# Output projection's second pass: reading S3's result ahead of the weight differences and the second half of the row combinations one product later; gate's S2 blocks split one step later

## The chip, the cores and the metric

The kernel runs on one core of one Trainium2 chip. The metric is the device time of one execution in microseconds (us), as the median of several runs of the same program; less is better. A separate execution was recorded by the hardware profiler; every row of a profile below comes from it. Engines are named as in the profile: PE is TensorE's matmul, PEld its weight load, DVE is VectorE, ACT is ScalarE, POOL is GpSimd, SP is SyncE, which here only issues transfers. A name with a q (SPq, ACTq) is the instruction queue of such an engine in a row about issues or waits.

## The reference

One decoder layer on 1024 tokens of 2048 features, all in float32. The part up to `mixed` is done before the place of the change; the change lies in the last lines but one.

```python
hn = rmsnorm(h, norm_mix_g[i])
proj = hn @ w_in[i]                       # q, k, v, gate columns of two head groups
...                                       # stick-breaking and differential attention
mixed = jnp.concatenate([sb_out * jax.nn.silu(sb_g), df_out * jax.nn.silu(df_g)], axis=-1)
h = h + mixed @ w_out[i]                  # 1024x2048 @ 2048x2048

gate = jax.nn.sigmoid(rmsnorm(h, norm_ple_g[i]) @ w_ple_gate[i])   # 2048x2048
h = h + gate * (p[i] @ w_ple_proj[i])     # 1024x256 @ 256x2048
...
return rmsnorm(h, norm_final_g)
```

## The kernel before

**Arithmetic.** All tiles hold features on the 128 partitions and 512 tokens (one half of the sequence) on the free axis. A float32 product is made of three matmuls of a shorter float format (fp32r): each operand is split into a high half, which ScalarE casts, and a low half, which VectorE gets by subtracting the high half from the original; TensorE then adds high by high, high by low and low by high into one accumulator.

**Seven products.** The projections and the gate go through a scheme of the Strassen kind (class `Seven`). The matrices are cut into two by two blocks, and instead of eight block products seven are made: A11 and A12, which take weight blocks as they are, S2, S1, S3 and S4, which take sums of operand rows (S1 to S4) and differences of weight blocks (T1 to T4) or a block itself, and A22, which takes T4. For the weights a block 12 is subtracted by a block 11 (T1), block 22 by T1 (T2), block 12 by 22 (T3), and block 21 by T2 (T4). Each product here is 12 matmuls of 128x512: four slices of the contraction, three matmuls each.

**The projection with w_out** runs in two passes over the contraction (`ph` 0 and 1) and in each over eight units (`u`), a unit being a group of 128 output features of each half. The second pass has seven products in a unit, in this order: A11, A22 of the unit before, S2, S4 of the unit before, A12, S1, S3. (Unit 7 has S3 ahead of S1.) Products of a unit are accumulated in few banks: S3 adds to the bank `b` in which S2 already lies, VectorE reads the two together as `u3 = b + s1` (L1912), and then A22 of the same unit accumulates into `b` again. The banks `b` and `c` bear the name `pbc`. The results, with what the first pass left (`hr`, read back from DRAM), are rows of the new h. `put` stores them to DRAM (`h_d`) from GpSimd and asks for their squares for the next RMSNorm: ScalarE squares (L1403), and for one half of the tokens GpSimd adds them up (`total`, L1404).

**The row combinations.** The gate needs sums of rows of h, S1 to S4, scaled with the norm's weights. The function `sums` makes them for one unit out of its four results and stores them to DRAM (`hcomb_d`). It has two halves: `one` (a ScalarE copy at L1791, VectorE's L1792 and L1794, two stores) and `two` (VectorE's L1798 and L1800, two stores). They are put into a list of deferred work, `soon`, with the number of the product after which they are to be issued: for units 0 to 5 at one and two products behind S4, for units 6 and 7 later.

**The step behind a product.** `prod` issues 12 matmuls and then calls `step`, which in this order: makes the high half of the next weights (`whigh`: for S2 and S3's places in the ring of weights it first subtracts T1 and T2, or T3, on VectorE at L764, and for A22 T4; then the cast on ScalarE at L799), calls `taken` (a function given by the caller, here the reading of S3's result), makes the low half (`wlow`, VectorE's L813), and runs the deferred work that is due. Weights are made one product ahead or more. A weight block's tile is loaded again from DRAM on SyncE's queue (`wload`, L1710 for the gate's, elsewhere for w_out's) as soon as its last reader has been issued; block 21 has one tile only, read by a cast and by T4.

**The gate** follows without a break. It takes its operands from `h_d` and `hcomb_d`: `gate_loads` issues the transfers at once and puts the splitting (cast at L684, low half later) into a queue `xq` with the earliest step. Its products are `gprod`: two steps of 12 matmuls each. Between them stands z, the embedding product of 12 matmuls with small weights `pwhl` (`ple`, L1859), whose cast at L1851 is issued by `plew` within `gate1`. `p1`, `p2` and `gate1` alternate: `p1(3)`, the loads of S2's first four blocks on ScalarE's queue, `p2(2)`, `gate1(0)`, `p1(4)`, `gate1(1)` and so on. ScalarE applies the sigmoid (L1990).

**The order of work.** On TensorE, VectorE and ScalarE the order is that in which the code issues the instructions in this stretch; each engine works its own list from top to bottom, and waits for other engines by semaphores. Transfers stand in the list of the engine that issues them. SyncE's and GpSimd's lists are set by a scheduler from the same program.

Of the kernel before, what the change touches and what calls it, by code (L numbers as in the profile page):

```python
# [70 lines left out]
def _body(ctx, nc, tc, ap):  # L71
# [551 lines left out]
    with tc.tile_pool(name="at", bufs=2) as at, ExitStack() as banks:  # L623
# [32 lines left out]
        class Seven:  # L656

            def __init__(self, w, n, flow):
                self.w, self.flow = w, flow
                self.units = [(ph, u) for ph in range(2) for u in range(n)]  # L660
                self.wq, self.XC, self.T = {}, {}, {}
                self.made, self.late, self.slot = [], 0, 0
                self.xq = deque()
                self.after = None
                self.soon, self.ended, self.calm, self.nlow = [], {}, False, 0
                self.extra, self.ticks = (), False
                self.ring, self.odd, self.opening = WRING, 1, list

            def places(self, place, nm):
# [163 lines left out]
            def step(self, taken=None):  # L833

                self.slot += 1
                self.whigh()
                if taken and not self.ticks:
                    taken()
                self.wlow()
                if self.slot in self.extra:  # L840
                    self.whigh()
                    self.wlow()
                self.due()
                if taken and self.ticks:
                    taken()
                for _ in range(3 if len(self.xq) > 8 and not self.calm else 2):
                    e = next((e for e in self.xq if e[0] <= self.slot), None)
                    if e:
                        self.xq.remove(e)
                        e[1]()  # L850

            def prod(self, u, ph, nm, o, start, taken=None):
                self.product(u, ph, nm, o, start, tick=self.ticks and bool(side.q))
                if u == 7 and self.ended:
                    for k in range(4):
                        del self.XC[nm, k]
                self.after(u, ph, nm)
                self.step(taken)
# [501 lines left out]
        def gate_operand(nm, i, eng):  # L1360

            hi, lo = op.places(GPLACE[nm][i], "g" + nm)
            src = {"A11": h_d[1, i], "A12": h_d[1, i + 8], "A22": h_d[0, i + 8]}.get(nm)
            if src is None:
                src = hcomb_d[SUMS.index(nm), i]
            gain = {"A11": i, "A12": i + 8, "A22": i + 8, "S3": i}.get(nm)
            if gain is not None:
                gain = gvec[:, 1, gain:gain + 1]
            if nm == "A12":
                with tc.issue_after(op.loaded.ins):  # L1370
                    eng.dma_start(lo.bitcast(F32), src)
            else:
                d = eng.dma_start(lo.bitcast(F32), src)
                if nm == "A11":
                    op.loaded = d
            return partial(op.split, "g" + nm, i, hi, lo, gain, apart=True)

        def gate_loads(nm, i0, n=4, eng=nc.sync):
            e = [(op.slot + (3 if nm in ("A11", "A12") else 2), gate_operand(nm, i0 + j, eng)) for j in range(n)]
            if nm == "A11" and i0 > 3:  # L1380
                xq.extendleft(reversed(e))
            else:
                xq.extend(e)
# [398 lines left out]
        def sums(u, hq, a2, b1):  # L1782

            a1, b2 = hq[:, 0, :], hq[:, 1, :]
            ga, ma, gb, mb = [g[:, k:k + 1] for k in (u, u + 8) for g in (gvec[:, 1, :], gneg)]

            def store(nm, v):
                nc.sync.dma_start(hcomb_d[SUMS.index(nm), u], v)

            def one():  # L1790
                A.activation(b2, b2, AF.Copy, scale=gb)  # L1791
                V.scalar_tensor_tensor(b2, a2, ga, b2, op0=ALU.mult, op1=ALU.add)  # L1792
                store("S1", b2)
                V.tensor_tensor(a2, a2, a1, op=ALU.subtract)  # L1794
                store("S3", a2)

            def two():
                V.scalar_tensor_tensor(a1, a1, ma, b2, op0=ALU.mult, op1=ALU.add)  # L1798
                store("S2", a1)
                V.scalar_tensor_tensor(b1, b1, mb, a1, op0=ALU.mult, op1=ALU.add)  # L1800
                store("S4", b1)

            return one, two
# [3 lines left out]
        def rest_of(st_, first):  # L1807

            u, ph, b, c, s1, u2, hq = st_
            nm, o_, t, hf, ch = ("A22", b, s1, 0, u) if first else ("S4", c, u2, 1, u + 8)  # L1810
            prod(u, ph, nm, o_, False)
            o = ftile()
            V.tensor_tensor(o, o_, t, op=ALU.add)
            put(o, ph, hf, ch)
            if ph == 1:
                hrows[u, hf] = o
                if not first:
                    lag = {6: 10, 7: 7}.get(u, 1)
                    op.soon.extend((op.slot + lag + i, fn) for i, fn in enumerate(sums(u, hq, hrows.pop((u, 0)), hrows.pop((u, 1)))))

        praws = []

# [38 lines left out]
                T.matmul(z, w[:, 1, k, :], ph[:, k, :], start=False, stop=k == 1)  # L1861

        for ph in range(2):
            op.ticks = not ph
            for u in range(8):
                r = {}
                for e in ((1, u + 8), (1, u), (0, u + 8), (0, u)) if ph else ():
                    r[e] = ev.tile([P, HALF], F32, name="hr", tag="xt", bufs=4)
                    nc.sync.dma_start(r[e], h_d[e])
                early = ph == 0 and u in s1s  # L1870
                s1 = s1s.pop(u) if early else ev.tile([P, HALF], F32, name="s1", tag="sq", bufs=2)
                if ph:
                    a = pp.tile([P, HALF], F32, name="pa", tag="acc", bufs=2)
                    prod(u, ph, "A11", a, True)
                    A.copy(s1, a)
                    if prev:
                        rest_of(prev, True)
                elif not early:
                    nc.sync.dma_start(s1, part_d[u])
                if ph == 0 and u % 3 == 0:  # L1880
                    b, c = [pp.tile([P, HALF], F32, name="pb", tag="acc", bufs=2) for _ in range(2)]
                elif ph == 1 and u == 7:
                    b = single("pbc")
                    c = None
                else:
                    b, c = single("pbc"), single("pbc")
                hq = at.tile([P, 2, HALF], F32, name="hq", tag="qz") if ph else None
                prod(u, ph, "S2", b, True)
                u2 = at.tile([P, HALF], F32, name="u2", tag="sg", bufs=3)
                V.tensor_tensor(u2, b, s1, op=ALU.add)  # L1890
                if ph:
                    V.tensor_tensor(u2, u2, r[1, u + 8], op=ALU.add)

                def p2():
                    prod(u, ph, "A12", a, False)
                    V.tensor_tensor(hq[:, 0, :], a, r[1, u], op=ALU.add)
                    put(hq[:, 0, :], ph, 1, u)

                if ph:
                    if prev:  # L1900
                        rest_of(prev, False)
                    p2()
                    if u < 7:
                        prod(u, ph, "S1", c, True)
                else:
                    if prev:
                        rest_of(prev, True)
                    prod(u, ph, "S1", c, True)
                    if prev:
                        rest_of(prev, False)  # L1910
                u3 = at.tile([P, HALF], F32, name="u3", tag="sg", bufs=3)
                prod(u, ph, "S3", b, False, lambda: V.tensor_tensor(u3, b, s1, op=ALU.add))  # L1912
                if ph:
                    V.tensor_tensor(u3, u3, r[0, u + 8], op=ALU.add)
                    if u == 7:
                        c = single("pbc")
                        prod(u, ph, "S1", c, True)
                o = hq[:, 1, :] if ph else ftile()
                V.tensor_tensor(o, c, u3, op=ALU.add)
                put(o, ph, 0, u + 8)  # L1920
                if ph:
                    V.tensor_tensor(s1, s1, r[0, u], op=ALU.add)
                prev = u, ph, b, c, s1, u2, hq
                if ph == 0 and 1 <= u < 5:
                    for nm, i in (("A11", u - 1), ("A12", u - 1)):
                        xq.append((op.slot + 3, load_operand(1, nm, i, A)))
# [495 lines left out]
```

## Time and profile before

| | |
|---|---|
| median of 3 runs | 2362.04 us (2360.44 to 2363.05) |
| profiled execution | 2361.19 us |
| its span, first to last instruction | 2359.4 us |
| mean granted TensorE clock | 0.997 |
| PE busy | 2317.2 us, 98% of the span, 11096 matmuls |
| PEld / DVE / ACT / POOL busy | 82% / 76% / 50% / 14% |
| chain of waits, by engine | PE 71%, DVE 12%, ACT 7%, DMA 6% |
| moved by DMA | 581.02 MB, mean 246 GB/s |

The span lies 1.8 us under the execution's own time: what stands around the first and the last instruction. In a row of a timeline the first number is the start in us from the start of the span, the second the duration in us, then engine, line, operation, output and inputs, and in brackets what the engine waited for ahead of it and how long. A row with x4 is four instructions of a kind in a row. In a row of the waits stand the microseconds in all, the number of waits and the longest. A row of windows has the stretch, its length, the busy times of PE, PEld, DVE, ACT and POOL with the number of instructions, the granted clock, the DMA engines' share of busy time, and GB/s. The second pass of the projection lies from about 1740 to 1985 us, unit by unit about 19 to 21 us apart; the gate follows.

### The profile page before, as it was taken

How to read it: one execution, taken by the hardware profiler on the slowest of the kernel's cores; microseconds unless marked ns; L12 is line 12 of the kernel's file. 1: busy time of each engine (PE TensorE's matmuls, PEld its weight loads, DVE VectorE, ACT ScalarE, POOL GpSimd, SP SyncE). 2: the span in 40 equal slices, each digit the busy share in tenths (PEclk: the TensorE clock that was granted, in tenths of full speed). 3: DMA queues.
4: the chain of work that ended last, by engine and by line, in shares of the span. 5: the costliest groups of instructions: out<-in, count | busy, mean ns of one | idle time of the engine just before them, and what ended most of it. 6: DMA issues, size and time to landing. Idle time of an engine off the chain costs nothing.

```text
span 2359.4 us, 32445 instructions
## 1 busy us (share of the span) xinstructions
PE 2317.2 (98%) x11096; PEld 1928.3 (82%) x11096; DVE 1789.8 (76%) x3123; ACT 1189.0 (50%) x2214; POOL 327.3 (14%) x480
## 2 busy tenths in 40 slices
PE   9999999999999999999999999999999999999997
PEld 7888888888888878887888888888878878788886
DVE  7489676666677787777888876767887877788778
ACT  6334243333367775445676764445633435533544
POOL 2211112332200000000001011011121232000000
PEclk9999999999999999999999999999999999999998
DMA  7699589999977788787656566677888778898666
GB/s 260 225 313 344 170 255 281 293 278 271 303 246 252 246 266 299 256 263 245 204 182 199 165 190 215 203 214 238 213 211 215 242 229 269 291 326 292 243 227 217
DMA packets 252725, 581.02 MB, mean 246 GB/s; under 512 B 28496, under 2 KB 41040, under 8 KB 252560
## 3 DMA queue, kind: packets, MB, share of 16 engines
q1 hardware_dynamic: 177952, 394.34, 49.7%
q0 software_dynamic: 55312, 149.71, 24.2%
q10 hardware_dynamic: 19296, 34.90, 4.3%
q8 instruction: 87, 1.43, 0.3%
q14 instruction: 78, 0.64, 0.1%
HBM read 373.32 MB, written 213.91 MB: 249 GB/s over the span
## 4 chain that ended last, share of the span: by engine, by line
PE 71%; DVE 12%; ACT 7%; DMA 6%; issue 3%; SPq 0%; ACTq 0%; DVEq 0%
PE acc L263 7%; PE acc L261 7%; PE acc L262 7%; PE pbc L708 6%; PE pbc L710 6%; PE pbc L709 6%; PE pa L708 2%; PE pa L710 2%; PE pa L709 2%; PE tp L480 2%; DMA wraw<-w_out 2%; PE pb L708 1%; PE pb L710 1%; PE pb L709 1%; PE pb L1941 1%
## 5 line engine op out<-in xcount | busy, mean ns | idle before, releaser
L799 ACT CAST wpr<-T 128x512 fp32r<-128x512 f32 x208 | 125.3, 621 | 440.3 <-DVE T L764 360.4
L261 PE MATMUL acc<-xh,whi 128*128 128x512 f32 x768 | 315.0, 410 | 0.0
L263 PE MATMUL acc<-xh,wlo 128*128 128x512 f32 x768 | 302.5, 394 | 1.5 <-DMA wlo<-wlo_d 1.4
L262 PE MATMUL acc<-xl,whi 128*128 128x512 f32 x768 | 301.0, 392 | 0.0
L263 PEld LDWEIGHTS acc<-xh,wlo 128*128 128x128 f32 x768 | 144.5, 188 | 36.2 <-DMA wlo<-wlo_d 3.6
L262 PEld LDWEIGHTS acc<-xl,whi 128*128 128x128 f32 x768 | 145.4, 189 | 24.0
L261 PEld LDWEIGHTS acc<-xh,whi 128*128 128x128 f32 x768 | 145.0, 189 | 23.4 <-DVE qk L1567 0.2
L799 ACT CAST wpr<-wraw 128x512 fp32r<-128x512 f32 x144 | 88.6, 618 | 146.9 <-DMA wraw<-w_vg 40.2
L813 DVE TENSOR_TENSOR wpr<-T,wpr 128x512 fp32r<-128x512 f32 x208 | 145.8, 701 | 9.2 <-ACT wpr L799 6.8
L936 POOL DMA_DIRECT2D vg_d<-hc x120 | 86.8, 724 | 328.4 <-DVE hc L1181 187.9
L503 DVE TENSOR_TENSOR awl<-tp,awh 128x256 fp32r<-128x256 f32 (+1 forms) x160 | 92.5, 578 | 42.8 <-ACT awh L498 42.2
L498 ACT CAST awh<-tp 128x256 fp32r<-128x256 f32 (+1 forms) x160 | 80.6, 504 | 82.6 <-PE tp L480 76.3
L813 DVE TENSOR_TENSOR wpr<-wraw,wpr 128x512 fp32r<-128x512 f32 x144 | 97.7, 686 | 23.5 <-ACT wpr L799 23.5
L321 DVE CUSTOM_DVE_ANT_0 z<-z,masks 128x512 f32<-128x512 f32 (+7 forms) x128 | 97.1, 769 | 23.0 <-PE z L341 14.0
L708 PE MATMUL pbc<-cS,wpr 128*128 128x512 f32 x288 | 112.0, 389 | 0.0
L709 PE MATMUL pbc<-cS,wpr 128*128 128x512 f32 x288 | 112.0, 389 | 0.0
L710 PE MATMUL pbc<-cS,wpr 128*128 128x512 f32 x288 | 112.0, 389 | 0.0
L373 DVE TENSOR_TENSOR_SCAN st<-pt 128x511 f32<-128x511 f32 (+3 forms) x64 | 86.7, 1354 | 27.2 <-ACT pt L366 26.8
L366 ACT ACTIVATE pt<-z 128x512 f32<-128x512 f32 (+3 forms) x64 | 41.8, 653 | 76.6 <-DVE z L349 74.6
L528 PE MATMUL av<-awl,v 128*128 128x256 f32 x256 | 73.4, 287 | 1.7 <-DVE awl L503 1.7
L526 PE MATMUL av<-awh,v 128*128 128x256 f32 x256 | 72.0, 281 | 0.7 <-ACT awh L498 0.7
L527 PE MATMUL av<-awh,v 128*128 128x256 f32 x256 | 72.2, 282 | 0.0
(589 smaller groups left out, 6816.5 us busy)
## 6 DMA issues: line engine op xcount, KB each, us to landing
wlo<-wlo_d SPq DMA_DIRECT2D x94, 512.0 KB, 5.2
whi<-whi_d SPq DMA_DIRECT2D x74, 512.0 KB, 4.1
wraw<-w_vg SPq DMA_DIRECT2D x129, 256.0 KB, 4.8
vg_d<-hc POOLq DMA_DIRECT2D x120, 256.0 KB, 5.7
wraw<-w_in SPq DMA_DIRECT2D x54, 512.0 KB, 5.3
wraw<-w_gate SPq DMA_DIRECT2D x92, 256.0 KB, 4.9
wraw<-w_out SPq DMA_DIRECT2D x72, 256.0 KB, 4.6
wlo_d<-wlo SPq DMA_DIRECT2D x34, 512.0 KB, 3.4
```

The source lines that it names most:

```text
L261: T.matmul(acc[c], hi[:, k2, kh, c, :], xh, start=first, stop=False)
L262: T.matmul(acc[c], hi[:, k2, kh, c, :], xl, start=False, stop=False)
L263: T.matmul(acc[c], lo[:, k2, kh, c, :], xh, start=False, stop=last)
L321: V.tensor_tensor_reduce(z, z, mwide[:, 0:n], -DF_SCALE, 3.0e38, ALU.add, ALU.min, mx)
L373: V.tensor_tensor_scan(st[:, off + 1:nkey], pt[:, off:nkey - 1], pt[:, off:nkey - 1], initial=1.0, op0=ALU.mult, op1=ALU.bypass)
L503: V.tensor_tensor(wl[:, o, :], tp[:, o, :], wh[:, o, :].bitcast(F32), op=ALU.subtract)
L708: T.matmul(o, wh[:, w], xh, start=start and k == 0, stop=False, skip_group_check=True)
L709: T.matmul(o, wh[:, w], xl, start=False, stop=False, skip_group_check=True)
L710: T.matmul(o, wl[:, w], xh, start=False, stop=k == 3, skip_group_check=True)
L799: A.copy(t[:, 0], src)
L813: V.tensor_tensor(t[:, 1], src, t[:, 0].bitcast(F32), op=ALU.subtract)
L936: G.dma_start(vg_d[hf, blk, u], o, **(dict(accum_op=ALU.add) if ph else {}))
```

## The change

Four edits, all in the order in which work is issued:

- In the projection's second pass (`op.first`), `step` calls `taken` ahead of `whigh`, not behind it: the reading of S3's result is issued before the next weights' differences.
- The second half of a unit's row combinations (`two`) is due two slots behind the first half instead of one, where the lag is 1 (the combinations of units 0 to 5, issued in units 1 to 6).
- In unit 7, where S1 follows S3, the reading of S1's result (now the function `second`) is given to `prod` as `taken`, instead of being issued after the whole step and after the sum with `r`.
- The gate's S2 blocks that ScalarE's queue loads first, `("S2", 0)`, may be split three steps after their issue, not two.

```diff
@@ -663,7 +663,7 @@
-                self.extra, self.ticks = (), False
+                self.extra, self.ticks, self.first = (), False, False
@@ -833,8 +833,10 @@
             def step(self, taken=None):
 
                 self.slot += 1
+                if taken and self.first:
+                    taken()
                 self.whigh()
-                if taken and not self.ticks:
+                if taken and not (self.ticks or self.first):
                     taken()
                 self.wlow()
                 if self.slot in self.extra:
@@ -1376,7 +1378,7 @@
         def gate_loads(nm, i0, n=4, eng=nc.sync):
-            e = [(op.slot + (3 if nm in ("A11", "A12") else 2), gate_operand(nm, i0 + j, eng)) for j in range(n)]
+            e = [(op.slot + (3 if nm in ("A11", "A12") or eng is A and (nm, i0) == ("S2", 0) else 2), gate_operand(nm, i0 + j, eng)) for j in range(n)]
@@ -1816,7 +1818,7 @@
                 if not first:
                     lag = {6: 10, 7: 7}.get(u, 1)
-                    op.soon.extend((op.slot + lag + i, fn) for i, fn in enumerate(sums(u, hq, hrows.pop((u, 0)), hrows.pop((u, 1)))))
+                    op.soon.extend((op.slot + lag + (1 + (lag == 1)) * i, fn) for i, fn in enumerate(sums(u, hq, hrows.pop((u, 0)), hrows.pop((u, 1)))))
@@ -1861,7 +1863,7 @@
         for ph in range(2):
-            op.ticks = not ph
+            op.ticks, op.first = not ph, ph
             for u in range(8):
@@ -1912,11 +1914,16 @@
                 prod(u, ph, "S3", b, False, lambda: V.tensor_tensor(u3, b, s1, op=ALU.add))
                 if ph:
                     V.tensor_tensor(u3, u3, r[0, u + 8], op=ALU.add)
-                    if u == 7:
-                        c = single("pbc")
-                        prod(u, ph, "S1", c, True)
                 o = hq[:, 1, :] if ph else ftile()
-                V.tensor_tensor(o, c, u3, op=ALU.add)
+
+                def second():
+                    V.tensor_tensor(o, c, u3, op=ALU.add)
+
+                if ph and u == 7:
+                    c = single("pbc")
+                    prod(u, ph, "S1", c, True, second)
+                else:
+                    second()
                 put(o, ph, 0, u + 8)
```

TensorE's and GpSimd's lists read the same before and after. Three places show what moves on the others. The line numbers of the changed kernel are two to seven higher there.

VectorE in a unit of the second pass, from the result of A12 to the result of S1. `hq` holds the unit's own results and, at L1798 (now L1800), those of the unit before; `u` is u3, `hc` a result of the unit before. Before:

```order
L1896 TENSOR_TENSOR hq<-pa,hr 128x512
L764 TENSOR_TENSOR T_18069<-wraw 128x512
L764 TENSOR_TENSOR T_18072<-wraw,T_18069 128x512
L813 TENSOR_TENSOR wpr<-wraw,wpr 128x512
L1798 SCALAR_TENSOR_TENSOR hq<-hq,gneg 128x512
L1800 SCALAR_TENSOR_TENSOR hc<-hc,gneg,hq 128x512
L1912 TENSOR_TENSOR u_18081<-pbc,s_17946 128x512
L813 TENSOR_TENSOR wpr<-T_18072,wpr 128x512
L1914 TENSOR_TENSOR u_18081<-u_18081,hr 128x512
L1919 TENSOR_TENSOR hq<-pbc,u_18081 128x512
```

After:

```order
L1898 TENSOR_TENSOR hq<-pa,hr 128x512
L764 TENSOR_TENSOR T_18069<-wraw 128x512
L764 TENSOR_TENSOR T_18072<-wraw,T_18069 128x512
L813 TENSOR_TENSOR wpr<-wraw,wpr 128x512
L1914 TENSOR_TENSOR u_18077<-pbc,s_17946 128x512
L813 TENSOR_TENSOR wpr<-T_18072,wpr 128x512
L1800 SCALAR_TENSOR_TENSOR hq<-hq,gneg 128x512
L1802 SCALAR_TENSOR_TENSOR hc<-hc,gneg,hq 128x512
L1916 TENSOR_TENSOR u_18077<-u_18077,hr 128x512
L1920 TENSOR_TENSOR hq<-pbc,u_18077 128x512
```

The two operations of `two` have gone behind the read of S3's result and one low half of weights. No difference of weights (L764) stands next to the read, before or after, so its place relative to those is unchanged in this unit; what has moved it is the edit of the slot.

ScalarE in the gate, around `gate1(0)`: the casts of weights (L799), of S2's operand blocks (L684, `cgS`), of the embedding's weights (`pwhl`), the sigmoid, and the copy behind `p1(4)`. Before:

```order
L799 CAST wpr<-wraw 128x512 x2
L684 CAST cgS_19147<-cgS_19147 128x512
L684 CAST cgS_19149<-cgS_19149 128x512
L1851 CAST pwhl<-pw 128x256
L799 CAST wpr<-wraw 128x512
L1990 ACT_TABLE_LOAD
L1990 ACTIVATE o<-o 128x512
L684 CAST cgS_19151<-cgS_19151 128x512
L684 CAST cgS_19153<-cgS_19153 128x512
L799 CAST wpr<-wraw 128x512
L2002 COPY s_19249<-paz 128x512
L2003 DMA part_d<-s_19249 128x512
```

After:

```order
L799 CAST wpr<-wraw 128x512 x2
L1853 CAST pwhl<-pw 128x256
L799 CAST wpr<-wraw 128x512
L1997 ACT_TABLE_LOAD
L1997 ACTIVATE o<-o 128x512
L684 CAST cgS_19147<-cgS_19147 128x512
L684 CAST cgS_19149<-cgS_19149 128x512
L799 CAST wpr<-wraw 128x512
L684 CAST cgS_19151<-cgS_19151 128x512
L684 CAST cgS_19153<-cgS_19153 128x512
L2009 COPY s_19247<-paz 128x512
L2010 DMA part_d<-s_19247 128x512
```

The first two S2 casts have gone behind the `pwhl` cast, the next weights' cast and the sigmoid; the third and fourth behind one more weight cast.

SyncE's list where the projection ends and the gate's loads begin. `cgA11l` are blocks of h for the gate's A11, `cgA12l` for A12, `wraw` the gate's weights. Before:

```order
L1710 DMA wraw<-w_gate 128x512
L1373 DMA cgA11l<-h_d 128x512
L1710 DMA wraw<-w_gate 128x512
L1710 DMA wraw_19487<-w_gate 128x512
L1710 DMA wraw<-w_gate 128x512
L1373 DMA cgA11l<-h_d 128x512
L1710 DMA wraw<-w_gate 128x512
L1371 DMA cgA12l<-h_d 128x512 x4
```

After:

```order
L1712 DMA wraw<-w_gate 128x512 x2
L1375 DMA cgA11l<-h_d 128x512 x3
L1712 DMA wraw<-w_gate 128x512 x2
L1712 DMA wraw_19487<-w_gate 128x512
L1712 DMA wraw<-w_gate 128x512 x2
L1375 DMA cgA11l<-h_d 128x512
L1373 DMA cgA12l<-h_d 128x512 x4
```

Ahead of the last `cgA11l` there now stand both weight loads that had one on each side of it, and three of the `cgA11l` are issued in a row.

## The prediction

> **What bounds the kernel now.** TensorE is busy nearly all the time, so I read first the list of waits on TensorE, to find the few that the change can reach.
>
> ```profile
> PE pbc L708 <- DVE u L1912: 3.5, 4, 1.5
> ```
>
> The columns are microseconds in all, times, and the longest. This is A22 of the projection's second pass: it accumulates into the bank that VectorE must first have read at L1912 (u3, the result of S3). Further down stands the small embedding product z in the gate, which waits for the cast of its weights:
>
> ```profile
> PE z L1859 <- ACT pwhl L1851: 1.5, 1, 1.5
> ```
>
> TensorE's timeline shows where the first wait falls (start, duration):
>
> ```profile
> 1861.02 0.39 PE L708 MATMUL pbc<-cA,wpr 128*128 128x512 f32 x1
> ...
> 1880.06 0.39 PE L708 MATMUL pbc<-cA,wpr 128*128 128x512 f32 x1
> ...
> 1920.34 0.50 PE L708 MATMUL pbc<-cA,wpr 128*128 128x512 f32 x1 [1.40 <-DVE u L1912]
> ...
> 1941.16 0.50 PE L708 MATMUL pbc<-cA,wpr 128*128 128x512 f32 x1 [1.46 <-DVE u L1912]
> ```
>
> A unit whose products are not held up takes 1880.06 - 1861.02 = 19.04 us. These are A22 after units 1, 2, 4 and 5. From 1880.06 to 1941.16 three units took 61.10 us, 3.98 more than 3 x 19.04. So the question is why VectorE falls behind by that much. Its own timeline, for unit 4 and the start of unit 5:
>
> ```profile
> 1913.70 1.28 DVE L1792 SCALAR_TENSOR_TENSOR hq<-hc,gvec,hq 128x512 f32<-128x512 f32 x1 [4.22 <-ACT hq L1791]
> ...
> 1918.15 0.74 DVE L1798 SCALAR_TENSOR_TENSOR hq<-hq,gneg 128x512 f32<-128x512 f32 x1
> 1918.93 0.75 DVE L1800 SCALAR_TENSOR_TENSOR hc<-hc,gneg,hq 128x512 f32<-128x512 f32 x1
> 1919.60 0.69 DVE L1912 TENSOR_TENSOR u<-pbc,s 128x512 f32<-128x512 f32 x1
> 1920.20 1.16 DVE L813 TENSOR_TENSOR wpr<-T,wpr 128x512 fp32r<-128x512 f32 x1
> 1921.29 0.68 DVE L1914 TENSOR_TENSOR u<-u,hr 128x512 f32<-128x512 f32 x1
> ...
> 1925.79 0.68 DVE L764 TENSOR_TENSOR T<-wraw,T 128x512 f32<-128x512 f32 x1
> ...
> 1934.52 1.28 DVE L1792 SCALAR_TENSOR_TENSOR hq<-hc,gvec,hq 128x512 f32<-128x512 f32 x1 [4.31 <-ACT hq L1791]
> ```
>
> TensorE resumed at 1920.34, 0.05 us after L1912 ended. From 1913.70 to 1925.79 VectorE stands still for nothing. The T at 1925.79 is T4; only when it has read block 21 may the next block 21 be loaded, and ScalarE's queue waits for that load:
>
> ```profile
> 1932.72 0.62 ACT L799 CAST wpr<-wraw 128x512 fp32r<-128x512 f32 x1 [4.55 <-DMA wraw<-w_out]
> ```
>
> Behind this cast, in ScalarE's order, stands L1791, and for that VectorE's next L1792 waits. This closes a loop: L1792, 12.09 us of VectorE work to T4, then 8.73 us of load and casts, L1792 again, 20.82 us in all. No step of it waits for TensorE. The loop, not the place of one read, is what is slower than 19.04 us.
>
> ```profile
> L1792 DVE SCALAR_TENSOR_TENSOR hq<-hc,gvec,hq x6: 1272/1276/1281, 1853.8 to 1954.1; 128x512 f32<-128x512 f32 x6
> ```
>
> The six L1792 of units 1 to 6 (durations in ns, first and last start): 100.3 us for five turns, 20.06 each.
>
> **The change part by part.** *u3 ahead of the row combinations (their second half one product later).* In units 1 to 6, L1798 and L1800 move behind L1912 and the following L813. L1912 can start where L1798 does, at 4.45 us after L1792 instead of 5.90: 1.45 us sooner. If the loop's turns keep their length, A22 after unit 6 is ready at 1954.11 + 4.45 + 0.69 + 0.05 = 1959.30. It now starts 0.05 us after L1912 as well, 1.45 us later. So the deadline is relieved once, by 1.45 us, and not in each unit: the waits do not go away, the loop runs late again. This is the upper end of that term if no turn becomes shorter.
>
> *What the move does to the turn.* GpSimd adds in the same place:
>
> ```profile
> 1919.49 1.33 POOL L1404 TENSOR_TENSOR total<-total,masks 128x512 f32<-128x512 f32 x1 [2.08 <-ACT masks L1403]
> ```
>
> L813 at 1920.20 overlaps this add and takes 1.16 us where the same subtraction's length elsewhere (L1914) is 0.68; it ends 0.54 us after the add. L1792 takes 1.28 against 0.74 of L1798. L1912, which reads the accumulator and one SBUF tile, lies wholly inside the add and keeps its 0.69. So the read of S3 covers about half of the add today. In the new order L1912 is at 4.45, L813 at 5.05, L1798 at 5.65 and L1800 at 6.4 after L1792, and the add is asked for at 5.79: it now meets only operations that it holds up. If L1798 has started, the add starts at its end near 6.3, lasts 1.3, and L1800 ends 0.54 us later, at 8.1; L1914 then starts at 8.05 instead of 7.59, 0.46 later in each turn. Bounds: 0.66 later (the add gets in ahead of L1798), 0.48 earlier (VectorE's back-to-back operations hold GpSimd off until L1914, so L813's present delay goes). I take 0.46, the case nearest to what the rows at L813 and L1792 show.
>
> [...]
>
> *The effect on the loop.* Five turns at +0.46 put L1792 of unit 6 at +2.3 us. A22 after unit 6 then starts at 1959.30 + 2.3 = 1961.6, 0.9 us later than now; in units 3 and 4 the 1.45 us still outweigh it.
>
> *Unit 7's S1 result read as soon as u3 is there.* On VectorE it passes one L813 and one L692. It removes at most about 0.3 us at S4 of unit 7, and this does not carry on (next part), so I cost it at nothing. "Read first" itself moves nothing in units 0 to 6: ahead of S3's step stands no weight difference on VectorE.
>
> *The loads at the seam.* SyncE's queue, before:
>
> ```profile
> 1980.11 0.33 SPq L1373 DMA_DIRECT2D cgA11l<-h_d  x1
> 1980.49 0.42 SPq L1710 DMA_DIRECT2D wraw<-w_gate  x1
> ```
>
> ```profile
> SPq L1373 <- DMA h_d<-hq: 3.7, 1, 3.7
> ```
>
> ```profile
> 1979.00:1981.00 2.00, 1.97 (x9) 1.33 (x8) 2.00 (x3) 1.29 (x3) 1.12 (x1) 1.00 0.08 30
> ```
>
> The last row's end is the DMA engines' busy share, 0.08, and GB/s: for two microseconds the engines are nearly empty, since the load at 1980.11 waits for a store of h to land. In the new order the weight load at 1980.49 stands ahead of it and fills the hole. That takes one 256 KB transfer out of the queue behind: at the page's mean rate 256 KB / 246 GB/s = 1.07 us, at a busier 300 or so 0.9; I take 0.9 sooner for the gate's loads.
>
> ```profile
> DMA packets 252725, 581.02 MB, mean 246 GB/s; under 512 B 28496, under 2 KB 41040, under 8 KB 252560
> ```
>
> *The gate's S2 blocks one step later.* ScalarE before:
>
> ```profile
> 2026.70 1.15 ACT L799 CAST wpr<-wraw 128x512 fp32r<-128x512 f32 x2 [2.73 <-DMA hc<-h_d]
> 2028.77 1.27 ACT L684 CAST cgS<-cgS 128x512 fp32r<-128x512 f32 x2 [0.93 <-DMA cgS<-hcomb_d]
> 2029.94 0.40 ACT L1851 CAST pwhl<-pw 128x256 fp32r<-128x256 f32 x1
> 2031.37 0.63 ACT L799 CAST wpr<-wraw 128x512 fp32r<-128x512 f32 x1 [1.03 <-DMA wraw<-w_gate]
> ...
> 2036.38 0.41 ACT L1851 CAST pwhl<-pw 128x256 fp32r<-128x256 f32 x1 [0.40 <-ACT s L2002]
> ```
>
> and TensorE, the held z, the product behind it, and the product behind the next z:
>
> ```profile
> 2030.40 0.50 PE L1859 MATMUL z<-ph,pwhl 128*128 128x512 f32 x1 [1.49 <-ACT pwhl L1851]
> ...
> 2031.90 0.40 PE L1939 MATMUL paz<-cgA12h,wpr 128*128 128x512 f32 x1
> ...
> 2039.13 0.39 PE L1939 MATMUL paz<-cgA11h,wpr 128*128 128x512 f32 x1
> ```
>
> The first pwhl is freed from the two S2 casts and can be done at 2028.2, so this wait goes. But the casts go from ScalarE's idle time to behind 2031.37, which waits for its own load; the next pwhl then ends 1.1 us later, at 2036.38 + 1.1 + 0.41 = 2037.9. With 0.05 for the release and 1.50 for a held z (2030.40 to 2031.90) the next product starts at 2039.45 instead of 2039.13. The wait moves to the next z, and what is left is 0.3 us of loss, whatever TensorE had gained before it, plus what the gate's loads have moved.
>
> *Sum.* At this z: loop +2.3 (the sixth turn's 0.46 falls into the two empty microseconds), weight load -0.9, second pwhl +0.3: +1.7 us. Behind it the DMA engines are full (row below; share 1.00 over 50 us), so what comes later passes on this shift and gives nothing back.
>
> ```profile
> 2045.00:2095.00 50.00, 50.00 (x222) 41.40 (x221) 38.91 (x65) 23.22 (x45) 0.00 (x0) 1.00 1.00 346
> ```
>
> The profiled execution took 2361.19 us; with the sum 2362.9. It lies 0.85 below the median of the three runs, 2362.04, so the median becomes 2363.7 us.
>
> **The rivals.** *No added hold-up on VectorE* (the turn stays at its length): the pass gains 1.45 us, but the second z binds: -0.9 + 0.3 = -0.6, 2361.4 us. For it: the add's start and L1798's differ by only 0.1 us. *VectorE keeps GpSimd off*: six turns 0.48 shorter, -2.9, with -0.9 and +0.3: -3.5, 2358.5 us. Nothing quoted shows GpSimd held over two operations. *All waits named above vanish*: 3.98 + 0.6 for units 3 to 6, 0.3 at unit 7 and 1.7 at z, 6.6 us, 2355.4 us. Against it: the loop, the second pwhl and the full DMA engines. *Slower:* the stores of S2 and S4 of each row combination leave 1.2 to 2.1 us later, so they share the DMA engines with the loads of hr and the next weights. If one 256 KB transfer lands ahead of block 21 in each of five turns, 5 x 1.07 = 5.3 us come on top of the 1.7: 2369 us. It decides once turns are longer than 21.9 us (20.82 + 1.07); against it, several microseconds pass between those stores and T4. [...]
>
> **How the numbers follow.** Forecast 0.50, no hold-up 0.22, GpSimd kept off 0.08, all waits gone 0.06, stores in the way 0.10, others 0.04 (split evenly). About 0.2%, 4.7 us, can be told from no change. Faster: 0.06 + 0.02 = 0.08; slower: 0.10 + 0.01, rounded 0.11; within: 0.81. The range takes in the first three cases with half a microsecond and the longer hold-up of 0.66 (five turns: +1.0) with scatter: 2358.2 to 2366.8. The forecast's own range is 2362.0 to 2365.5.
>
> **What would show it.** Right: L1912 4.45 us after L1792; L1798 or L1800 near 1.3 us and longer together than 1.5, the L813 behind L1912 back at 0.68; L1792 to L1792 still 19.5 to 21.3 us; TensorE still waiting for u3 late in the pass; the wait at the first z gone or below 0.5 us and one of 2 us or more at the second. Wrong: turns near 19.04 us, no wait of TensorE for u3, and no wait at the second z: then the loop follows TensorE after all, and the full gain appears.

## The result

The changed kernel takes 2365.47 us (median of 22 runs, 2361.87 to 2369.86), the kernel before 2362.03 us (22 runs beside them, 2356.35 to 2363.78). The ratio is 1.0018, 95% interval 1.0012 to 1.0024, that is 2.8 to 5.7 us slower. The forecast was 2363.7 us, slightly slower and within what a single measurement can tell from no change; the loss is twice as large as forecast by the medians (3.4 for 1.7 us), and two and a half times by the ratio.

The profiled execution of the changed kernel has a span of 2365.6 us, 6.2 us over that of the kernel before. Not all of it belongs to the change. Both kernels issue the same 11096 matmuls in the same order, so the two traces can be lined up matmul by matmul; the drift of a matmul is its start in the changed kernel less that in the kernel before. The changed kernel already starts the second pass 3.44 us later (1724.61 and 1728.05 for the same matmul), in code that is the same in both; the profiled executions of the kernels below differ there from the kernel before by -1.6 to +3.1 us. Of the 3.44, 1.5 arise at 907 us (last section). What the change did in this pair of executions is in the drift behind that point:

| place | before | after | drift less 3.44 |
|---|---|---|---|
| A22 after unit 4 | 1920.34 | 1923.91 | +0.13 |
| A22 after unit 5 | 1941.16 | 1945.49 | +0.89 |
| first S2 matmul behind it | 1944.01 | 1949.81 | +2.36 |
| A22 after unit 6 | 1960.74 | 1966.14 | +1.96 |
| first gate product | 1982.96 | 1987.90 | +1.50 |
| first z (the one that waited before) | 2030.40 | 2033.68 | -0.16 |
| product behind the second z | 2039.13 | 2043.13 | +0.56 |
| gate's S4, unit 1 | 2119.10 | 2123.68 | +1.14 |
| last quarter's A22 | 2322.07 | 2328.06 | +2.55 |

The wait for u3 that the change aimed at has not gone, it has grown: 4.1 us in the changed kernel's list of waits in the second pass and the gate's start (1860 to 2050 us), 3.5 before. The one at the first z has been replaced by one at the second:

```profile
PE pbc L708 <- DVE u L1914: 4.1, 3, 2.2
PE z L1861 <- ACT pwhl L1853: 1.0, 1, 1.0
```

VectorE's timeline in the changed kernel, the unit that answers to the one shown of before (L1794 is the former L1792, L1914 reads u3, L1800 and L1802 are the second half of the combinations):

```profile
1918.72 1.28 DVE L1794 SCALAR_TENSOR_TENSOR hq<-hc,gvec,hq 128x512 f32<-128x512 f32 x1 [3.87 <-ACT hq L1793]
...
1923.18 0.68 DVE L1914 TENSOR_TENSOR u<-pbc,s 128x512 f32<-128x512 f32 x1
1923.78 0.68 DVE L813 TENSOR_TENSOR wpr<-T,wpr 128x512 fp32r<-128x512 f32 x1
1924.37 0.75 DVE L1800 SCALAR_TENSOR_TENSOR hq<-hq,gneg 128x512 f32<-128x512 f32 x1
1925.16 1.65 DVE L1802 SCALAR_TENSOR_TENSOR hc<-hc,gneg,hq 128x512 f32<-128x512 f32 x1
...
1931.23 0.68 DVE L764 TENSOR_TENSOR T<-wraw,T 128x512 f32<-128x512 f32 x1
...
1940.30 1.28 DVE L1794 SCALAR_TENSOR_TENSOR hq<-hc,gvec,hq 128x512 f32<-128x512 f32 x1 [4.65 <-ACT hq L1793]
```

and GpSimd's add in the same unit:

```profile
1924.51 1.75 POOL L1406 TENSOR_TENSOR total<-total,masks 128x512 f32<-128x512 f32 x1 [2.08 <-ACT masks L1405]
```

u3 is read 4.46 us behind L1794 and not 5.90 behind it. But L1802 takes 1.65 us, T4 stands 12.51 us behind L1794 (12.09 before), and the next L1794 comes 21.58 us after this one (20.82 before). Over all units, the groups of L1794 and L1802 from 1850 to 1965 us (minimum, median and maximum duration in ns, first and last start):

```profile
L1794 DVE SCALAR_TENSOR_TENSOR hq<-hc,gvec,hq x6: 1274/1280/1286, 1856.7 to 1960.5; 128x512 f32<-128x512 f32 x6
...
L1802 DVE SCALAR_TENSOR_TENSOR hc<-hc,gneg,hq x5: 752/1654/1668, 1865.0 to 1946.7; 128x512 f32<-128x512 f32 x5
```

Five turns took 103.8 us, 20.76 each; before it was 20.06. With VectorE later by that much, the longest stall at A22 went from 1.46 to 2.22 us, and something followed it that the trace of before had not shown in this place:

```profile
1945.49 0.79 PE L708 MATMUL pbc<-cA,wpr 128*128 128x512 f32 x1 [2.22 <-DVE u L1914]
1946.08 0.63 PE L709 MATMUL pbc<-cA,wpr 128*128 128x512 f32 x1
...
1948.21 0.60 PE L708 MATMUL pbc<-cA,wpr 128*128 128x512 f32 x1
1948.64 0.42 PE L709 MATMUL pbc<-cA,wpr 128*128 128x512 f32 x1
1948.89 0.39 PE L710 MATMUL pbc<-cA,wpr 128*128 128x512 f32 x1
```

For 3 us the matmuls start 0.43 us apart, not 0.227, and the profile's granted clock from 1945.5 to 1948.6 us is 0.50: TensorE ran at half its clock. That cost 1.5 us, the step from +0.89 to +2.36 in the table.

### The profile page after: what moved, and what is told of

It reads as the page before. It is cut to its first block, busy times and chain, and to the rows that moved or that the text cites. A ratio compares the mean times of both kernels' runs of the same rounds, so it can differ in the third digit from the quotient of the medians.

```text
span 2365.6 us, 32440 instructions
## 1 busy us (share of the span) xinstructions
PE 2320.7 (98%) x11096; PEld 1932.0 (82%) x11096; DVE 1792.1 (76%) x3123; ACT 1188.5 (50%) x2214; POOL 329.8 (14%) x480
## 4 chain that ended last, share of the span: by engine, by line
PE 74%; DVE 11%; DMA 7%; ACT 6%; issue 2%; SPq 0%; ACTq 0%; DVEq 0%
PE acc L263 7%; PE acc L261 7%; PE acc L262 7%; PE pbc L708 7%; PE pbc L710 7%; PE pbc L709 7%; PE pa L708 2%; PE pa L710 2%; PE pa L709 2%; PE tp L480 2%; PE pb L710 1%; PE pb L708 1%; PE pb L709 1%; DMA wraw<-w_out 1%; DMA wlo<-wlo_d 1%
## 5 line engine op out<-in xcount | busy, mean ns | idle before, releaser
L799 ACT CAST wpr<-T 128x512 fp32r<-128x512 f32 x208 | 125.4, 622 | 449.4 <-DVE T L764 365.4
L799 ACT CAST wpr<-wraw 128x512 fp32r<-128x512 f32 x144 | 88.6, 618 | 139.1 <-DMA wraw<-w_vg 46.4
L813 DVE TENSOR_TENSOR wpr<-T,wpr 128x512 fp32r<-128x512 f32 x208 | 143.7, 691 | 9.1 <-ACT wpr L799 6.7
L813 DVE TENSOR_TENSOR wpr<-wraw,wpr 128x512 fp32r<-128x512 f32 x144 | 98.8, 693 | 23.7 <-ACT wpr L799 23.7
```

The source lines that it names most:

```text
L799: A.copy(t[:, 0], src)
L813: V.tensor_tensor(t[:, 1], src, t[:, 0].bitcast(F32), op=ALU.subtract)
```

## The experiments

Times are medians; each ratio is to runs of the kernel before on the same chip.

### The row combinations one product later, alone

```diff
-op.soon.extend((op.slot + lag + i, fn) ...
+op.soon.extend((op.slot + lag + (1 + (lag == 1)) * i, fn) ...
```

> Only the second half of the row combinations one product later; reading first, unit 7's S1 and the gate's S2 split as before. Theory (the move lengthens VectorE's turn, because GpSimd's add now meets the combinations): the last combination lasts about 1.65 us instead of 0.75, T4 stands 12.5 us behind L1792 instead of 12.1, and TensorE still waits for u3 in units 3 to 5, 3.5 to 6 us in all; the weight load at the seam moves with this edit. The first z keeps its wait of 1 to 1.5 us. Time 2363 to 2366 us. Rival (the gate's edit is what costs): u3 waits go, time 2358 to 2361.5 us.

2363.16 us against 2361.40, ratio 1.0011 (1.0003 to 1.0020). VectorE's, GpSimd's and SyncE's lists of the second pass are then those of the changed kernel (unit 7's S1 apart), the order at the seam too. The last combination and the turns are as in the changed kernel, and so are the waits for u3 in its list of waits:

```profile
L1800 DVE SCALAR_TENSOR_TENSOR hc<-hc,gneg,hq x6: 752/1667/1670, 1861.7 to 1963.8; 128x512 f32<-128x512 f32 x6
L1792 DVE SCALAR_TENSOR_TENSOR hq<-hc,gvec,hq x6: 1273/1278/1284, 1853.4 to 1957.3; 128x512 f32<-128x512 f32 x6
PE pbc L708 <- DVE u L1912: 4.3, 3, 2.3
```

A turn is 20.78 us. The 2.3 us stall was followed by half clock again, which cost 1.6 us. By the ratios this edit carries 2.6 of some 4.2 us, the larger part of the loss, as far as the intervals tell. One thing in the expectation was wrong: the first z did not keep its wait. TensorE came to it some 2.9 us later (a drift of 3.49 us behind unit 7's S4, less 0.62 at 1724), and by then pwhl was ready.

### The gate's S2 blocks a step later, alone

```diff
-e = [(op.slot + (3 if nm in ("A11", "A12") else 2), ...
+e = [(op.slot + (3 if nm in ("A11", "A12") or eng is A and (nm, i0) == ("S2", 0) else 2), ...
```

> Only the gate's first S2 blocks split a step later. Theory (the wait moves from the first z to the second): the first z's 1.5 us wait is gone, the second z waits 1 to 2 us, and the DMA engines and VectorE behind it, which are full, take back what is left: 2361 to 2363 us. Rival (this edit is what makes the changed kernel slower): 2364 to 2366 us.

2361.80 us against 2361.40, ratio 1.0003 (0.9994 to 1.0013): no change that can be told. In its list of waits, from 1860 to 2090 us:

```profile
PE z L1859 <- ACT pwhl L1851: 1.1, 2, 0.7
```

The first z waits no more; the second waits 0.70 us and the one at 2081.86 0.37. The wait has moved, as the theory said, though it is smaller than the 1 to 2 us expected. The two edits together give 2.6 + 0.7 us by their ratios, which agrees with the 2.8 to 5.7 us of the whole change; but either edit alone already takes the first z's wait away, so the two need not add up. The edit in unit 7 was not tried by itself.

### GpSimd's adds left out, with the change and without it

```diff
             else:
                 A.activation(spare32, o, AF.Square)
-                G.tensor_tensor(totals[1], totals[1], spare32, op=ALU.add)
```

> The changed kernel without GpSimd's fifteen adds of squares (total), so the norm's sum over one half of the tokens lacks all rows but one; ScalarE's squares stay. Theory (the add holds up VectorE): L1794 and L1802 last 0.75 us instead of 1.28 and 1.65, T4 stands at about 11.1 us behind L1794 instead of 12.5, a turn falls from 20.8 to 19.1 to 19.6 us, TensorE's waits for u3 fall from 4.1 us to under 1 us; 2360 to 2363 us by what the gate gives back. Rival (the longer turn is from the loads and stores): durations change, but turns stay at 20.3 us or more and the u3 waits stay at 3 us or more, 2364 to 2366 us.

> The kernel before without GpSimd's adds of squares (the norm's sum over one half of the tokens lacks all rows but one). Theory (the add's hold-up is what the change made larger; without adds the two orders are alike): L1792 0.75 us, T4 11.1 us behind L1792 as in the changed kernel without adds, turns of 19.0 to 19.7 us, u3 waits under 1 us in all, 2357 to 2360.5 us. Rival (the later row combinations cost by something else than the add): T4 stays 0.4 us apart from the changed kernel without adds, or this kernel is faster than that one by 2 us or more.

With the change 2357.77 us, ratio 0.9983 (0.9974 to 0.9993); without it 2356.58 us, ratio 0.9983 (0.9974 to 0.9992). Without the adds the two kernels are alike, and both are faster than the kernel before, by a little more than was expected. The groups of the changed kernel without adds (L1793 and L1801 there), then that of the kernel before without adds (L1791):

```profile
L1793 DVE SCALAR_TENSOR_TENSOR hq<-hc,gvec,hq x6: 750/751/752, 1856.4 to 1952.5; 128x512 f32<-128x512 f32 x6
...
L1801 DVE SCALAR_TENSOR_TENSOR hc<-hc,gneg,hq x6: 751/752/754, 1863.6 to 1958.8; 128x512 f32<-128x512 f32 x6
```

```profile
L1791 DVE SCALAR_TENSOR_TENSOR hq<-hc,gvec,hq x6: 750/751/752, 1854.7 to 1949.2; 128x512 f32<-128x512 f32 x6
```

1280 ns have become 751 and 1654 ns 752; T4 stands 11.08 us behind L1793 or L1791 wherever VectorE does not wait for TensorE, in both. Turns are 19.22 and 18.90 us, and no wait for u3 is left in either list. What the operations cost with an add beside them is thus the add's doing, and the loss of the slot edit as well: it put both combinations where the add falls.

### T4 made early: with the change, without it, and without the slot edit

T4 is the last reader of weight block 21. Here it is made right behind T2's low half, in the slot of S3. In unit 4 of the kernel before with this edit it stands 7.81 us behind L1796 (the former L1792), where it stood at 12.09: 4.3 us earlier, and the next block 21 is loaded that much sooner.

```diff
                     self.todo.append(((u, ph, nm), nm == "S4", fns[n][nm],
-                        partial(self.wload, n + 2, 22) if nm == "S4" else None))
+                        partial(self.wload, n + 2, 22) if nm == "S4" else self.then2.get(n) if nm == "S2" else None))
...
+                if self.soon_t4 and self.units[n][0]:
+                    self.then2[n] = t4
                 return {"A11": lambda: self.B[11], "A12": lambda: self.B[21], "S2": t2, "S1": lambda: t["T1"],
-                        "S3": t3, "S4": lambda: b22_, "A22": t4}
+                        "S3": t3, "S4": lambda: b22_, "A22": (lambda: t["T4"]) if n in self.then2 else t4}
```

> The changed kernel with T4, the last reader of weight block 21, made on VectorE right behind T2's low half (6 us earlier), so that the next block 21 is loaded 6 us sooner. Theory (the loop over block 21's load and ScalarE's queue sets the turn): ScalarE's waits of 4 to 5 us for w_out's block go, L1794 no longer comes late, turns fall to 19.04 us and the waits for u3 go: 2359 to 2362 us. Rival (VectorE's work or the hold-up itself sets the turn): turns stay above 20 us, the waits for u3 stay, 2364 to 2367 us.

> The kernel before with T4 made right behind T2's low half, and none of the change's edits. Theory (the loop over block 21's load sets the turn): the waits for u3 go as in the changed kernel with this edit, though u3 is read behind the row combinations; the first z keeps a wait of 1 to 1.7 us: 2358.5 to 2361.5 us, within 1.5 us of the changed kernel with T4 early (2359.4). Rival (reading u3 ahead of the combinations is what is needed once the load is out of the way): u3 waits of 0.5 us or more in most units, 2361 to 2363 us.

> The changed kernel with T4 early and the row combinations back in their old slot (unit 7's S1 and the gate's S2 split as changed). Theory: u3 waits gone in units 1 to 6, last combination 0.75 us, no wait at the first z, 0 to 1 us at the second: 2358 to 2361 us, the same within 1.5 us as the changed kernel with T4 early (2359.4). Rival (the change's slot edit is a gain once the loop is broken): slower than that by 1.5 us or more, with u3 waits.

| | us | ratio to before |
|---|---|---|
| changed kernel, T4 early | 2359.39 | 0.9987 (0.9979 to 0.9996) |
| kernel before, T4 early | 2357.53 | 0.9989 (0.9979 to 0.9998) |
| changed kernel, T4 early, combinations in the old slot | 2358.67 | 0.9991 (0.9981 to 1.0002) |

The kernel before with this one edit computes the same and beats both kernels. Its groups and its waits in the second pass and the gate's start are:

```profile
L1796 DVE SCALAR_TENSOR_TENSOR hq<-hc,gvec,hq x6: 1284/1362/1492, 1850.8 to 1946.3; 128x512 f32<-128x512 f32 x6
PE pbc L709 <- DVE hq L1923: 0.8, 1, 0.8
```

A turn is 19.10 us, TensorE's own unit, though the add's hold-up is still there (1284 ns and more where 751 would do) and u3 is still read behind the combinations. ScalarE's waits of 4 to 5 us for block 21 are gone, and with them every wait for u3. The wait at the first z, which was expected to stay, has gone too: from the pass's start to the gate's S4 of unit 1 this profile gained 7.0 us on that of before (the drift there is -8.54, that at 1724 -1.58). The median gained 3.75 us, 2.6 by the ratio. Between the three the differences are within their intervals, so once the loop is broken neither the slot edit nor the gate's edit can be told to do anything. With the change one new wait stands in unit 7:

```profile
PE pbc L709 <- DVE u L1918: 1.7, 1, 1.7
```

There u3 stands behind a low half whose cast waits for the gate's first weights, 5.10 us by ScalarE's timeline: what is late next is a load of the gate.

### The squares added by DMA

```diff
-                A.activation(spare32, o, AF.Square)
-                G.tensor_tensor(totals[1], totals[1], spare32, op=ALU.add)
+                t = ev.tile([P, HALF], F32, name="rsq1", tag="rstd1", bufs=1) if nsq1[0] % 2 else spare32
+                A.activation(t, o, AF.Square)
+                G.dma_start(sq_d[2 + nsq1[0] % 2], t, **(dict(accum_op=ALU.add) if nsq1[0] > 1 else {}))
```

> The changed kernel with the second half's squares added up by accumulating DMAs to DRAM (as the other half's are) and read back ahead of the norm, in place of GpSimd's adds: same result. Theory (the hold-up comes from the add on GpSimd, not from what it adds): L1794 and the last combination 0.75 us, T4 11.1 to 11.3 us behind L1794, u3 waits under 1.5 us in all; the 16 more accumulating transfers take some of it back in the loads: 2358 to 2363 us. Rival (the added transfers hold up block 21's load as much as the adds held up VectorE): turns of 20.3 us and more, u3 waits of 3 us or more, 2364 to 2368 us.

2364.89 us, ratio 1.0016 (1.0007 to 1.0025). The theory was right on VectorE and wrong on the time, which lies in the rival's range, though the turns are not the rival's. The operations are short, and a turn is 19.75 us; u3 cost TensorE 0.8 us in units 3 to 6. But the transfers came back elsewhere. The windows from 1860 to 1960 us, of the kernel before and then of this one, whose last two numbers are the DMA engines' share and GB/s:

```profile
1860.00:1960.00 100.00, 96.79 (x425) 79.16 (x424) 81.45 (x120) 36.58 (x65) 32.96 (x41) 1.00 0.80 233
```

```profile
1860.00:1960.00 100.00, 99.19 (x437) 81.53 (x436) 77.91 (x123) 37.33 (x67) 28.64 (x41) 1.00 0.95 262
```

With the engines at 0.95, the gate's first weights came late:

```profile
1975.10 0.62 ACT L799 CAST wpr<-wraw 128x512 fp32r<-128x512 f32 x1 [6.49 <-DMA wraw<-w_gate]
```

and u3 of unit 7, behind them on VectorE, held TensorE for 2.72 us, with half clock after it. Stage by stage, the pass gained 3.2 us up to unit 6 and gave back 4.3 at the seam.

### Matmuls in the stall

```diff
+            if ph and first and u in (4, 5):
+                d = pp.tile([P, HALF], F32, name="fill", tag="t")
+                xh = op.XC["A22", 0][0]
+                for _ in range(6):
+                    T.matmul(d, xh[:, 0:P], xh, start=True, stop=True, skip_group_check=True)
```

> The changed kernel with six 128x512 matmuls into an unused bank (1.4 us of TensorE in all, their result is never read) ahead of A22 after units 4 and 5, where TensorE stood for 1.5 and 2.2 us. Theory (the longer stall in unit 5 lets the granted clock fall to half for about 3 us, which costs 1.5 us more): the stalls left behind the six are 0.1 to 1 us, A22 starts no later than it did, no matmuls at 0.43 us spacing stand behind it; the pass ends 1 to 1.6 us sooner than in the changed kernel's trace; mean granted clock 0.996 or 0.997 in nearly all runs, 2363 to 2365 us. Rival (the slow matmuls were chance or come from something else than the stall): matmuls at half clock stand there again, or the six only push A22 back: 2365 to 2368 us.

2364.77 us, ratio 1.0012 (1.0003 to 1.0021). This one is inconclusive. In its profile no half clock follows A22 after units 4 and 5:

```profile
1941.23 1.52 PE L1817 MATMUL fill<-cA 128*128 128x512 f32 x6
1942.68 0.50 PE L708 MATMUL pbc<-cA,wpr 128*128 128x512 f32 x1
1943.02 0.40 PE L709 MATMUL pbc<-cA,wpr 128*128 128x512 f32 x1
```

But in this execution the loads were quicker (ScalarE's waits for block 21 in units 4 and 5 are 4.02 and 3.92 us, 4.10 and 4.88 in the changed kernel), so that there was no stall left behind the six matmuls, and the turns (20.54 us) were shorter too. The mean granted clock was 0.995 in 4 of 12 runs, no fewer than in the changed kernel. The median lies in the first theory's range, near its end, but the granted clock that this theory expected in nearly all runs is not there.

## Why the prediction was right, and where it was not

The time lies in the stated range, and only just in the forecast's own (2365.47 of 2362.0 to 2365.5); by the ratio, some 4.2 us, it would lie above that one. The direction and the mechanism of the loop were right. The sum was not, and that it came out near is in part luck: at the place where it was worked out, behind the second z, the profile has a third of it, and the rest arose where nothing had been forecast.

*What bounds the kernel: the loop.* Right. It was read from the row in which ScalarE's cast waits for block 21, and the experiment that loads this block earlier took the turn from 20.06 to 19.10 us and all waits for u3 away, while u3 was read in its old place. "The loop, not the place of one read" holds.

*u3 ahead: 1.45 us, once.* Right in size: L1914 stands 4.44 to 4.46 us behind L1794 in units 2 to 6. In unit 1 it stands at 5.26, since S3 was not done: here the read came before its data, and VectorE waited 0.7 us for TensorE. "No step of it waits for TensorE" was true of the old order only. This lengthened the first turn.

*The hold-up.* Right: 1.65 to 1.67 us for L1802 in units 2 to 5, T4 12.52 us behind L1794 where it stood at 12.09 to 12.12 in three of these four units, 0.42 later (0.46 forecast), and L813 behind u3 back at 0.68. That the add is the cause is shown by the kernels without it (1654 ns with it, 752 without). In unit 4 the add, which starts while L1800 runs, is recorded as 1.75 us long, where those of before from 1850 to 1965 us took 1.27 to 1.42, and L1802 ends 0.55 us after it; in units 2, 3 and 5 it is 0.54 to 0.55 us. By what means the two hold each other up is not shown.

*The effect on the loop.* Right in kind, too small: a turn grew by 0.70, not 0.46. T4 stood 0.57 later on average (1.35 in the first turn, 0.41 to 0.43 in three, 0.22 in the last), and the way from T4 to the next L1794 took 0.13 more. A22 after unit 6 drifted by +1.96. There the half clock, not u3, held it; u3 was ready at 1965.66, so without the half clock it would still have been +1.48, where 0.9 was forecast.

*Not foreseen: half clock.* The step "A22 after unit 6 then starts ..." counted a stall as its own length. The longest stalls of the pass cost more: in this profile and in that of the slot edit alone those of 2.22 and 2.34 us were followed by half clock, 1.5 to 1.6 us more each. How often this happens in unprofiled runs can only be seen coarsely: the mean granted clock, given to three places, was 0.994 or 0.995 in 6 of 22 runs of the changed kernel and in 2 of 85 runs of the kernel before beside the experiments. Half clock for 3 us lowers the mean by 3 x 0.5 / 2360 = 0.0006; the two means differ by 0.0006. By that estimate the changed kernel has about one such spell in a run more, 1.5 us. That it is the one behind A22 is not shown: the kernel before with T4 early, in whose profile no stall in the pass is longer than 0.8 us, has 0.995 in 3 of 11 runs. Nor does it show how much of a spell reaches the end of the kernel; in this profile it was swallowed at z (below).

*Unit 7's S1.* Costed at nothing, a gain of 0.2 to 0.3 us at S4 (the drift falls by 0.19 there). Right.

*The seam.* The weight loads now stand in a row ahead of the load that waits for its store, and the two microseconds before that one is issued are full, by the window's last two numbers. A window laid around the issue as the prediction's was (1985.02 to 1987.02) has 0.59 and 226 GB/s, where it had 0.08 and 30:

```profile
1973.95 8.78 SPq L1712 DMA_DIRECT2D wraw<-w_gate  x5
1986.13 0.33 SPq L1375 DMA_DIRECT2D cgA11l<-h_d  x1
```

```profile
1984.00:1986.00 2.00, 2.00 (x10) 1.65 (x10) 2.00 (x4) 2.00 (x4) 0.00 (x0) 1.00 1.00 392
```

Here the sum has its mis-sized term. ScalarE's cast in the gate that waits for its load starts at 2035.13, 0.3 us later than before after taking off the 3.44, where the loop's loss less the load's gain, 2.3 less 0.9, had been put at 1.4. The loop's loss was no smaller: L1794 of unit 6 came 2.9 us late by the same measure. So 2.6 us were regained on the way, not 0.9. The order of the loads was not tried by itself, so how much of this it did stays open.

*z.* Right in direction, wrong in size. The rows of the changed kernel:

```profile
2031.59 0.40 ACT L1853 CAST pwhl<-pw 128x256 fp32r<-128x256 f32 x1
2035.13 0.62 ACT L799 CAST wpr<-wraw 128x512 fp32r<-128x512 f32 x1 [3.14 <-DMA wraw<-w_gate]
...
2041.17 0.40 ACT L1853 CAST pwhl<-pw 128x256 fp32r<-128x256 f32 x1 [0.40 <-ACT s L2009]
```

```profile
2041.63 0.50 PE L1861 MATMUL z<-ph,pwhl 128*128 128x512 f32 x1 [0.98 <-ACT pwhl L1853]
...
2043.13 0.39 PE L1946 MATMUL paz<-cgA11h,wpr 128*128 128x512 f32 x1
```

The first z is free, the second waits, and the product behind it starts 1.50 us after it, as worked out. But the wait is 0.98 us, not 2 or more. The smaller part of this is TensorE, which came to it 0.3 us sooner than in the kernel before, where the forecast's terms give 0.6. The larger part is that the weights were ready 1.2 us sooner than forecast, nearly all of it by the cast at 2035.13. From this cast on the sum was right: +0.3 for the load and +0.3 for the two casts give +0.6, and the product behind the second z drifted by +0.56, where the sum said +1.7. Since z waited for ScalarE here, the half clock behind A22 no longer shows in what follows, as far as this profile tells. One phrase was too wide: the 0.3 us are not left "whatever TensorE had gained before it". With TensorE earlier, as in the kernels with T4 early, the loads that this chain on ScalarE waits for came earlier as well, and the second z waited little or not at all.

*"What comes later passes on this shift."* Wrong. Another 0.6 us came where VectorE is full, 9.96 of 10 us from 2105 to 2115 us (waits of 0.32 and 0.70 us there, one of 0.44 before), and 1.4 at the end of the gate:

```profile
PE pbq L2261 <- DVE qt L2268: 1.3, 1, 1.3
```

There ScalarE's cast of the last weight block, which waits for its load, starts at 2319.62, before at 2313.27: 1.8 us later when the 4.58 of drift up to there are taken off, though SyncE's list of transfers is the same there. This wait is in the profiles of six of the other nine kernels as well: in four of the five that have the slot edit, 0.5 to 1.2 us, and in two of the four without it, 0.2 and 0.8 us. What sets it stays open.

The sum, +1.7 us, thus has one term too large, the loads of the gate at 1.4 for 0.3, and lacks what is behind the gate's start, 2.0 of the profile's 2.55. Over all runs it is 2.8 to 5.7; that the median of 22 runs is made up as this one profile is, is not shown. Of the rivals, "no hold-up" is refuted by the 1.65 us, "GpSimd kept off" and "all waits vanish" too, and the stores did not hold up block 21 by a transfer: the way from T4 to the next L1794 grew by 0.13 us, not by 1.07.

## What to carry to other kernels

When an engine holds up TensorE by being late, ask what makes it late before moving the one operation that TensorE waits for: here the chain went from VectorE's order through the last reader of a weight block, its reload and ScalarE's queue back to VectorE, and moving that last reader gave 2.6 us (3.75 by the medians) where moving the awaited read gave a loss. Work put off to "one slot later" lands beside something else; look at what GpSimd does in that slot: here the combination beside its add ended 0.55 us after the add and took 1.65 us for 0.75. And a stall of TensorE may cost more than its length, if nothing later makes TensorE wait anyway: the three of 2.22 to 2.72 us in the second pass were all followed by half clock, and so was the one of 2.80 us at 907 us in six of eleven profiles, for 1.3 to 1.7 us each.

## What the runs showed that was not expected

The half clock. In eleven profiles, the same stall of 2.80 us at about 907 us was followed by matmuls 0.43 us apart in six, and by none in the five others. One of each kind, of the kernel before and of the changed kernel:

```profile
907.23 0.47 PE L261 MATMUL acc<-cA11h,whi 128*128 128x512 f32 x1 [2.80 <-DVE qk L1567]
907.54 0.39 PE L262 MATMUL acc<-cA11l,whi 128*128 128x512 f32 x1
```

```profile
907.88 0.77 PE L261 MATMUL acc<-cA11h,whi 128*128 128x512 f32 x1 [2.80 <-DVE qk L1569]
908.44 0.63 PE L262 MATMUL acc<-cA11l,whi 128*128 128x512 f32 x1
```

Of the stalls in the second pass, those of 2.22, 2.34 and 2.72 us were all followed by it, and none of those up to 1.69 us; one of 1.7 us at 830 us was in two of eleven, and one of 1.3 to 1.8 us at 1080 us, behind short transposes, in eight. Each spell lasts about 3 us and costs 1.3 to 1.7 us. What decides whether a stall is followed by half clock is not shown: the same stall of 2.80 us was so in some executions only, while one of 2.22 us in the second pass was enough.
